# FFN gate and up in a transformer block: half of the k-tiles in pairs by a Strassen form, with sums of weights on GpSimd

## The chip, the cores and the metric

One core of a Trainium2 chip runs one launch of the kernel. The metric is the device time of the launch in microseconds (us), the median of the runs shown.

## The reference

One layer over 256 tokens of width 2,048, all in float32: an input projection, differential attention and a state-space branch side by side, a merge, an output projection, and then the part that the change touches, the feed-forward network (FFN):

```python
z = _rms_norm(h, norm_ffn_pre[l])
f = (jax.nn.silu(z @ w_ffn_gate[l]) * (z @ w_ffn_up[l])) @ w_ffn_down[l]
h = h + _rms_norm(f, norm_ffn_post[l])
```

`w_ffn_gate` and `w_ffn_up` are 2048 x 5632, `w_ffn_down` is 5632 x 2048.

## The kernel before

The kernel is a list of blocks (class `Block`). A block multiplies 256 tokens, as two halves t of 128, with weights that come in k-tiles of 128 rows and 1,024 columns. A weight tile is loaded in float32 (`do_load`, line 178), then split (`do_split`, line 191): ScalarE rounds it to fp32r, `hi`, and VectorE forms `lo` = raw - hi. Activations are split in the same way. A product is then three matmuls into one PSUM bank, hi x hi, hi x lo and lo x hi (`run_block`, line 254).

The FFN's gate and up are eleven blocks, ffn0 to ffn10 (lines 1266 to 1276). Block b takes columns 512 b to 512 b + 511 of both matrices: a raw tile holds 512 gate columns and beside them 512 up columns (`load_ffn`, line 1233), so it comes by two DMAs, or, where a tile for two k-tiles is used, by two larger ones. There are 16 k-tiles, two token halves and two column halves c (gate, up): 16 x 4 products, 192 matmuls of 128x512, in four accumulators of one bank each. `ffn_evac` (line 1243) takes Silu of the gate bank on ScalarE and multiplies with the up bank on VectorE; the root-mean-square factor of the norm is put in there, as a scale per token. `hid_t` (line 1257) transposes the result with eight matmuls per block into `hT`, which the block "down" reads.

What sets the order: `ensure` (line 210) asks, ahead of step i, for the splits up to step i + 4 and for loads up to eight further steps. There are five buffers each for hi and lo in this stage (three in `ring`, two in `late`), so split i + 5 uses the buffers of split i and can't start before TensorE is through with that. Raw tiles come from a ring of four, and at two places in eight from a pool of six large buffers (`big8`), as a tile for two k-tiles. From the ninth step of ffn0 on (`unpin`), a scheduler may move instructions within their engines; what it made of it is the order shown below. GpSimd has nothing to do in the eleven blocks but one small power (`make_rstd`, line 393).

The normalised activations are made at the end of the output projection and in ffn0: `h_transpose` (line 1176) puts transposed pieces into the scratch tile `ga`, `h_split` (line 1187) splits them into `zT`. PSUM has eight banks: four in the pool `acc`, two single ones in `side`, and one double one (`side2`).

```python
        A.copy(h, raws[i])
        V.tensor_tensor(l, raws[i], h.bitcast(F32), op=ALU.subtract)
```

Of the kernel before, what the change touches and what calls it, by code (L numbers as in the profile page):

```python
# [88 lines left out]
def hybrid_block_kernel(  # L89
# [85 lines left out]
    state = dict(loaded=0, split=0, cap=None)  # L175
    raws, his, los = {}, {}, {}

    def do_load(i):
# [12 lines left out]
    def do_split(i):
# [1023 lines left out]
    def norm2():  # L1215
# [9 lines left out]
        before={12: lambda: cap(wo1, 17, True), 13: lambda: cap(wo1, 17, True), 16: lambda: cap(wo1, 18), 17: lambda: h_transpose(0, 0)},  # L1225
        post=wo_post)
# [40 lines left out]
    for b in range(NB):  # L1267
        pre = None
        if b == 1:
            def pre():  # L1270
                w_ = big8()
                A.dma_start(w_, norm_ffn_post.broadcast_to([P, DM]))
                wpost2.append(w_)
        add(f"ffn{b}", 16, load_ffn(b), lz, ffn_evac(b), budget=0.6, pre=pre,
            )
    blocks[-NB].order = token_order(16, head=4)[:8] + bank_order(16)[4:]
# [148 lines left out]
```

## Time and profile before

| what | value |
|---|---|
| median of 3 runs | 1437.61 us (1437.18 to 1438.76) |
| the profiled execution | 1436.86 us |
| its span | 1435.1 us |
| busy share of the span | PE 96%, DVE 64%, ACT 47%, POOL 16% |
| granted clock of TensorE, mean | 0.985 |
| bytes moved by DMA | 266.7 MB, mean 186 GB/s |

PE is TensorE, DVE VectorE, ACT ScalarE, POOL GpSimd, SP SyncE, which issues most DMAs. The span is the time from the first to the last instruction of the execution that was profiled; the execution's own time is 1.8 us longer. Times in the views count from the start of the span. An instruction's listed time runs from its start on its engine to its end, a wait for a shared resource after the start included.

### The profile page before, as it was taken

Reading aid. Unit: us, or ns where it says so; the run is one execution under the profiler, and the core shown is the slowest. Engines: PE = TensorE matmul, PEld = TensorE weight load, DVE = VectorE, ACT = ScalarE, POOL = GpSimd, SP = SyncE. Lnnn points to the kernel's source line nnn. Section 1 sums busy time; section 2 is a strip of 40 time slices with the busy share of each in tenths; the row PEclk is TensorE's granted clock in tenths of the full one; section 3 lists DMA queues with packets and bytes.
Section 4 is the critical chain, followed back from the end, with each engine's and each line's share of the span. In section 5 each row is a group of like instructions: output and inputs, shape, how many; then the busy total and the mean of one; then the engine's idle time right before and its main releaser. Section 6 shows DMA issues by size and latency. Waiting matters only on the chain.

```text
span 1435.1 us, 17346 instructions
## 1 busy us (share of the span) xinstructions
PE 1375.7 (96%) x6367; PEld 1115.7 (78%) x6367; DVE 923.2 (64%) x1122; ACT 680.8 (47%) x989; POOL 232.9 (16%) x195
## 2 busy tenths in 40 slices
PE   8998898999899879999999999999999999999997
PEld 6887676668676659888788888888888888888885
DVE  5965999967999975754764444444444445555555
ACT  4654443497443354444464444444444435444443
POOL 3293545500645500000000000000000000000001
PEclk9999999999999999999999999999999999999999
DMA  8688555444456465655576555556565564555651
GB/s 259 187 263 253 171 175 154 141 132 140 154 158 176 145 184 207 227 197 191 188 238 202 197 182 196 176 191 205 176 199 185 175 211 171 204 200 182 205 176 59
DMA packets 102006, 266.70 MB, mean 186 GB/s; under 512 B 10176, under 2 KB 17168, under 8 KB 98528
## 3 DMA queue, kind: packets, MB, share of 16 engines
q1 hardware_dynamic: 100704, 260.09, 56.1%
q10 hardware_dynamic: 608, 4.20, 0.8%
q0 software_dynamic: 608, 1.30, 0.4%
q8 instruction: 50, 0.82, 0.2%
q14 instruction: 36, 0.29, 0.1%
HBM read 257.16 MB, written 8.39 MB: 185 GB/s over the span
## 4 chain that ended last, share of the span: by engine, by line
issue 55%; PE 23%; DVE 15%; ACT 3%; DMA 2%; SPq 1%; POOL 0%; POOLq 0%; DVEq 0%; ACTq 0%
PE acc L41 22%; DVE lo L41 4%; DVE ssA L41 2%; DVE ssB L41 2%; DVE ssD L41 2%; PE side L41 2%; DVE ssC L41 2%; DMA raw<-in_w_in_dram 1%; DVE sim L41 1%; ACT hi L41 1%; SPq L623 1%; DMA raw<-in_w_glu_dram 1%; ACT prob L41 1%; DVE sre L41 1%; DVE b L41 1%
## 5 line engine op out<-in xcount | busy, mean ns | idle before, releaser
L41 DVE TENSOR_TENSOR lo<-raw,hi 128x1024 fp32r<-128x1024 f32 (+1 forms) x341 | 439.7, 1294 | 246.5 <-ACT hi L41 243.0
L41 ACT CAST hi<-raw 128x1024 fp32r<-128x1024 f32 (+1 forms) x340 | 355.0, 1051 | 399.0 <-PE acc L41 316.8
L41 PE MATMUL acc<-lo,zT_h 128*128 128x512 f32 x704 | 275.1, 391 | 0.0
L41 PE MATMUL acc<-hi,zT_l 128*128 128x512 f32 x704 | 274.3, 390 | 0.0
L41 PE MATMUL acc<-hi,zT_h 128*128 128x512 f32 x704 | 271.2, 393 | 0.2 <-ACT zT_h L41 0.2
L41 DVE TENSOR_TENSOR lo<-b,hi 128x1024 fp32r<-128x1024 f32 x124 | 151.1, 1224 | 147.6 <-ACT hi L41 147.6
L41 PE MATMUL acc<-lo,xT_h 128*128 128x512 f32 x512 | 207.4, 408 | 14.1 <-DVE lo L41 14.1
L41 PE MATMUL acc<-hi,xT_l 128*128 128x512 f32 x512 | 202.0, 397 | 0.0
L41 ACT CAST hi<-b 128x1024 fp32r<-128x1024 f32 x124 | 130.6, 1053 | 120.4 <-PE acc L41 104.0
L41 PE MATMUL acc<-hi,xT_h 128*128 128x512 f32 x512 | 165.8, 407 | 5.8 <-ACT hi L41 4.1
L41 PEld LDWEIGHTS acc<-hi,zT_h 128*128 128x128 f32 x704 | 132.3, 188 | 27.6 <-ACT zT_h L41 0.7
L41 PEld LDWEIGHTS acc<-hi,zT_l 128*128 128x128 f32 x704 | 132.3, 188 | 27.6
L41 PEld LDWEIGHTS acc<-lo,zT_h 128*128 128x128 f32 x704 | 132.3, 188 | 26.5
L41 PEld LDWEIGHTS acc<-lo,xT_h 128*128 128x128 f32 x512 | 98.8, 193 | 44.2 <-DVE lo L41 22.4
L41 PEld LDWEIGHTS acc<-hi,xT_h 128*128 128x128 f32 x512 | 97.6, 194 | 29.2 <-ACT hi L41 5.1
L41 PEld LDWEIGHTS acc<-hi,xT_l 128*128 128x128 f32 x512 | 98.3, 192 | 20.1 <-issue 0.8
L398 POOL TENSOR_TENSOR rstdf<-rstdfm,half 128x1 f32<-128x1 f32 x2 | 1.1, 546 | 691.6 <-DVE rstdfm L41 691.6
L41 PE MATMUL acc<-hi,b 128*128 128x512 f32 x256 | 84.1, 403 | 1.3 <-DVE ga L41 1.0
L638 POOL TENSOR_TENSOR tabS<-tabs,tabc 128x512 f32<-128x512 f32 x16 | 46.9, 2932 | 143.9 <-DVE ssB L41 143.9
L41 PE MATMUL acc<-lo,hTh 128*128 128x512 f32 x176 | 68.5, 389 | 0.0
L41 PE MATMUL side<-lo,hTh 128*128 128x512 f32 x176 | 68.5, 389 | 0.0
L41 PE MATMUL side<-hi,hTh 128*128 128x512 f32 x176 | 68.5, 389 | 0.0
(209 smaller groups left out, 1796.0 us busy)
## 6 DMA issues: line engine op xcount, KB each, us to landing
raw<-in_w_in_dram SPq DMA_DIRECT2D x127, 512.0 KB, 3.9
raw<-in_w_ffn_gate_dram SPq DMA_DIRECT2D x96, 256.0 KB, 2.8
raw<-in_w_ffn_up_dram SPq DMA_DIRECT2D x96, 256.0 KB, 3.1
raw<-in_w_ffn_down_dram SPq DMA_DIRECT2D x44, 512.0 KB, 3.7
b<-in_w_ffn_down_dram SPq DMA_DIRECT2D x22, 1024.0 KB, 4.9
b<-in_w_ffn_gate_dram SPq DMA_DIRECT2D x40, 512.0 KB, 3.8
b<-in_w_ffn_up_dram SPq DMA_DIRECT2D x40, 512.0 KB, 4.7
raw<-in_w_out_dram SPq DMA_DIRECT2D x32, 512.0 KB, 4.1
```

Of the source, the lines that this page charges most:

```text
L41: ins = f(*a, **kw)
L398: G.tensor_tensor(r, ms, half[:, :n], op=ALU.pow)
L623: nc.sync.dma_start(stack_b[:, j // 2, n, :, j % 2].rearrange("g q o n -> q g o n"), t_[32 * j:32 * j + 32])
L638: G.tensor_tensor(tss, hi(sa), lo(cb), op=ALU.mult)
```

## The change

In ffn1 to ffn10 the 16 k-tiles become four groups of four: two direct tiles (D), and a pair. For a pair the products form a 2 x 2 matrix of blocks: rows are the token halves, the inner index is the two k-tiles, columns are gate and up. Instead of eight block products it uses seven, in the Strassen-Winograd form. They need four sums of weight blocks of 128x512, t1 = b12 - b11, t2 = b22 - t1, t3 = b22 - b12, t4 = b21 - t2, which GpSimd forms in half of `ga` (`do_sums`). What is split for a pair is R2 (the second raw tile, two products), B1 (the gate half of the first, one product), T13 (t1 and t3, two) and T24 (t2 and t4, two): 24 splits in a block, four of them half as wide, where there were 16. Direct tiles still have four products, though one of them uses the difference of the two token halves' activations, so that all tiles add into the same seven accumulators P1 to P7. `combos` forms the sums of activations, once, during ffn0. At a block's end `s_evac` makes the four results out of the seven banks with seven additions and a copy, then Silu and gating from SBUF. Seven of the eight banks are in use in a block; odd and even blocks lay them out differently (`s_alloc`). The other half of `ga` holds the raw pairs of every second group, the four ring buffers everything else, and `big8` loads are used no more in ffn1 to ffn10 nor in the first eight steps of down. The load of the last norm's weights moves from ffn1 to the ninth step of down.

```diff
     def do_split(i):
...
-        A.copy(h, raws[i])
-        V.tensor_tensor(l, raws[i], h.bitcast(F32), op=ALU.subtract)
+        if blk.sets and blk.sets[k][0] != "D":
+            kind, kk = blk.sets[k]
+            r1, r2 = blk.pairs[kk]
+            raw = dict(R2=r2, B1=r1[:, 0:512], T13=sums[:, 0:1024], T24=sums[:, 1024:2048])[kind]
+        else:
+            raw = raws.pop(i)
         his[i], los[i] = h, l
-        del raws[i]
+        h, l = h[:, 0:raw.shape[1]], l[:, 0:raw.shape[1]]
+        A.copy(h, raw)
+        V.tensor_tensor(l, raw, h.bitcast(F32), op=ALU.subtract)
+
+    def do_sums(i):
...
+        t1, t3, t2, t4 = (sums[:, 512 * n:512 * n + 512] for n in range(4))
+        G.tensor_tensor(t1, b12, b11, op=ALU.subtract)
+        if kind != "T24":
+            G.tensor_tensor(t3, b22, b12, op=ALU.subtract)
+        G.tensor_tensor(t2, b22, t1, op=ALU.subtract)
+        G.tensor_tensor(t4, b21, t2, op=ALU.subtract)
+        if kind == "T24":
+            G.tensor_tensor(t3, b22, b12, op=ALU.subtract)
 
     def ensure(i):
...
+        while state["summed"] <= min(hi_i + 2, len(flat) - 1, state["loaded"] - 1):
+            do_sums(state["summed"])
+            state["summed"] += 1
...
+    def combos(cb):
...
+        tt(z1[:, k0:k1], z0[:, k0:k1], z1[:, k0:k1], op=ALU.subtract)
+        tt(z1[:, k2], z1[:, k1], z1[:, k2], op=ALU.add)
+        tt(z1[:, k1], z0[:, k1], z1[:, k1], op=ALU.subtract)
+        tt(z0[:, k1], z1[:, k2], z0[:, k1], op=ALU.subtract)
+        tt(z0[:, k2], z0[:, k2], z0[:, k1], op=ALU.subtract)
+        (ch, cl), cd = hold["cs"], hold["cd"]
+        for src, h, l in ((z1[:, k0:k1], cd[:, 0, cb], cd[:, 1, cb]),
+                          (z1[:, k1:k1 + 2], ch[:, 0:2, cb], cl[:, 0:2, cb]),
+                          (z0[:, k1:k1 + 2], ch[:, 2:4, cb], cl[:, 2:4, cb])):
+            A.copy(h, src)
+            tt(l, src, h.bitcast(F32), op=ALU.subtract)
...
+    for q in range(4):
+        SETS += [("D", 4 * q), ("D", 4 * q + 1)]
+        SETS += [(kind, 4 * q + 2) for kind in (("R2", "B1", "T13", "T24") if q < 3 else ("T24", "B1", "T13", "R2"))]
+    USES = dict(D=(("P4", 0), ("P5", 1), ("P2", 0), ("P3", 1)), R2=(("P2", 0), ("P3", 1)), B1=(("P1", 0),),
+                T13=(("P7", 1), ("P5", 0)), T24=(("P6", 0), ("P4", 1)))
...
+    def s_evac(b):
+        def f(key, accs):
...
+            if key == "P1":
+                A.copy(s0, accs["P1"])
+                plus(X, s0, "P6")
+            elif key == "P7":
+                plus(Y, X, "P7")
+            elif key == "P5":
+                plus(X, X, "P5")
+            elif key == "P3":
+                plus(X, X, "P3")
+                plus(s1, Y, "P4")
+                plus(Y, Y, "P5")
+                plus(s0, s0, "P2")
+                gated(1, s1, Y)
+                gated(0, s0, X)
...
+    for b in range(1, NB):
+        add(f"ffn{b}", len(SETS), load_ffn(b), None, s_evac(b), budget=0.6, mm=s_mm, alloc=s_alloc(b),
+            order=[[(n, key, c) for key, c in USES[kind]] for n, (kind, _) in enumerate(SETS)])
+        blocks[-1].sets = SETS
```

How the instructions now stand on three engines follows. In the rows, `raw`, `ga` and `b` numbers tell buffers apart, and the brackets name the engines or DMA queues that a row waits for.

GpSimd, from the end of the state-space tables to the end of the program, before:

```order
L640 TENSOR_TENSOR tabS_4270<-tabS_4270,tabt_874_4271 128x512 [waits Pool_49]
L398 TENSOR_TENSOR rstdm_5910<-rstdmm_5908,half 128x1 [waits DVE_49]
L398 TENSOR_TENSOR rstdm_5953<-rstdmm_5951,half 128x1 [waits DVE_49]
L398 TENSOR_TENSOR rstdh_6251<-rstdhm_6249,half 128x2 [waits DVE_49]
L398 TENSOR_TENSOR rstdf_11152<-rstdfm_11150,half 128x1 [waits DVE_49]
```

GpSimd in ffn1 now, the four sums of one pair from ring buffers and of one from `ga`:

```order
L243 TENSOR_TENSOR ga<-raw_6457 128x512 [waits DMAHW5_49,DMAHW4_49,DVE_49]
L245 TENSOR_TENSOR ga<-raw_6458,raw_6457 128x512 [waits DMAHW7_49]
L246 TENSOR_TENSOR ga<-raw_6458,ga 128x512 [waits DVE_49,Pool_49]
L247 TENSOR_TENSOR ga<-raw_6458,ga 128x512 [waits DMAHW6_49,Pool_49]
L243 TENSOR_TENSOR ga<-ga 128x512 [waits DMAHW3_49,DMAHW2_49,DVE_49]
L249 TENSOR_TENSOR ga<-ga 128x512 [waits DMAHW1_49]
L246 TENSOR_TENSOR ga<-ga 128x512 [waits DVE_49,Pool_49]
L247 TENSOR_TENSOR ga<-ga 128x512 [waits DMAHW0_49,Pool_49]
```

Where GpSimd had no work between two norms it has 16 subtractions per block, and each group of sums waits for VectorE's splits of the group before, whose place in `ga` it takes.

VectorE at the end of ffn1, before (b is the tile of the gate values, acc the banks):

```order
L41 TENSOR_TENSOR lo_6615<-raw_6465,hi_6614 128x1024 [waits DMAHW3_49,DMAHW2_49,Activation_49]
L41 TENSOR_TENSOR lo_6637<-raw_6484,hi_6636 128x1024 [waits DMAHW5_49,DMAHW4_49,Activation_49]
L41 SCALAR_TENSOR_TENSOR b_1155_5959<-acc_6373,rstdh_6251,b_1155_5959 128x512 [waits PE_49,Activation_49]
L41 SCALAR_TENSOR_TENSOR b_1155_5959<-acc_6375,rstdh_6251,b_1155_5959 128x512 [waits PE_49,Activation_49]
L41 TENSOR_TENSOR lo_6641<-raw_6503,hi_6640 128x1024 [waits DMAHW7_49,DMAHW6_49,Activation_49]
L41 TENSOR_TENSOR lo_6691<-b_1248_6522,hi_6690 128x1024 [waits DMAHW1_49,DMAHW0_49,Activation_49]
```

VectorE at the end of ffn1 now (acc_6414 to acc_6417 are P4, P5, P2, P3; side_1220 holds P6 and P7; lo_6738, lo_6750 and lo_6783 are R2, B1 and T13 of the next block's first group):

```order
L41 TENSOR_TENSOR b_1046_5329<-b_1046_5329,side_1220_6413 128x512 [waits Activation_49]
L41 TENSOR_TENSOR lo_6738<-raw_6626,hi_6737 128x1024 [waits DMAHW6_49,DMAHW7_49,PE_49,Activation_49]
L41 TENSOR_TENSOR b_1046_5329<-b_1046_5329,acc_6416 128x512 [waits DVE_49,PE_49]
L41 TENSOR_TENSOR lo_6750<-raw_6625,hi_6749 128x512 [waits DMAHW4_49,Activation_49]
L41 TENSOR_TENSOR b_1046_5329<-b_1046_5329,side_1220_6413 128x512 [waits PE_49]
L41 TENSOR_TENSOR lo_6783<-ga,hi_6782 128x1024 [waits Activation_49]
L41 TENSOR_TENSOR b_1046_5329<-b_1046_5329,acc_6415 128x512 [waits DVE_49]
L41 TENSOR_TENSOR b_1046_5329<-b_1046_5329,acc_6414 128x512
L41 TENSOR_TENSOR b_1046_5329<-b_1046_5329,acc_6417 128x512 [waits DVE_49]
L41 TENSOR_TENSOR b_1046_5329<-b_1046_5329,acc_6415 128x512 [waits DVE_49]
L41 SCALAR_TENSOR_TENSOR b_1046_5329<-b_1046_5329,rstdh_6290 128x512 [waits DVE_49,Activation_49] x2
```

Two gatings from PSUM became seven additions from PSUM and two gatings from SBUF, and three of the additions stand between splits of the next block.

ScalarE in ffn2 between the two copies into hT and after, before:

```order
L41 COPY hT<-side_1270_6672 128x4x128 [waits PE_49]
L41 CAST hi_6706<-b_1248_6522 128x1024 [waits DVE_49,PE_49]
L41 CAST hi_6725<-b_1253_6557 128x1024 [waits DMAHW2_49,DMAHW3_49,DVE_49,PE_49]
L41 COPY hT<-side_1270_6672 128x4x128 [waits PE_49]
L41 CAST hi_6741<-b_1253_6557 128x1024 [waits DVE_49,PE_49]
L41 CAST hi_6760<-raw_6592 128x1024 [waits DMAHW4_49,DMAHW5_49,DVE_49,PE_49]
```

ScalarE at the same place now (hi_6807 is T24 of the first group, hi_6833 and hi_6843 the direct tiles of the second, hi_6873 and hi_6892 its T13 and T24, hi_6926 a direct tile of the third):

```order
L41 COPY hT<-side_6767 128x4x128 [waits PE_49]
L41 CAST hi_6807<-ga 128x1024 [waits PE_49,Pool_49]
L41 CAST hi_6833<-raw_6672 128x1024 [waits DMAHW4_49,DMAHW3_49,PE_49]
L41 CAST hi_6843<-raw_6691 128x1024 [waits DMAHW6_49,DMAHW5_49,PE_49]
L41 COPY hT<-side_6798 128x4x128 [waits PE_49]
L41 CAST hi_6926<-raw_6804 128x1024 [waits DMAHW1_49,DMAHW2_49,DVE_49,PE_49]
L41 CAST hi_6873<-ga 128x1024 [waits DVE_49,PE_49,Pool_49]
L41 CAST hi_6892<-ga 128x1024 [waits DVE_49,PE_49,Pool_49]
L41 CAST hi_6916<-raw_6779 128x1024 [waits DMAHW0_49,DMAHW7_49,DVE_49,PE_49]
```

Casts of sums wait for GpSimd, and hi_6926 was moved ahead of three casts of sets that come earlier in the block.

## Rows read from the trace of the kernel before

**Rows 1.** The page: busy time, share, instructions; granted clock in 40 slices.

```profile
PE 1375.7 (96%) x6367; PEld 1115.7 (78%) x6367; DVE 923.2 (64%) x1122; ACT 680.8 (47%) x989; POOL 232.9 (16%) x195
...
PEclk9999999999999999999999999999999999999999
```

**Rows 2.** Windows of ffn0 and of two later blocks, with granted clock and DMA.

```profile
core 0: us, PE busy (x) PEld busy (x) DVE busy (x) ACT busy (x) POOL busy (x), PEclk, DMA share, GB/s
692.80:737.30 44.50, 44.41 (x208) 36.42 (x209) 35.07 (x46) 26.18 (x44) 1.53 (x2) 1.00 0.74 252
780.77:825.26 44.49, 44.49 (x201) 36.84 (x200) 20.84 (x19) 19.32 (x21) 0.00 (x0) 1.00 0.56 189
825.26:869.75 44.49, 44.49 (x201) 36.85 (x200) 20.86 (x19) 19.32 (x21) 0.00 (x0) 1.00 0.58 189
```

**Rows 3.** Timeline of ACT: start, duration, instruction, idle time before it.

```profile
760.37 1.05 ACT L41 CAST hi<-raw 128x1024 fp32r<-128x1024 f32 x1 [1.67 <-DMA raw<-in_w_ffn_up_dram]
763.09 1.05 ACT L41 CAST hi<-b 128x1024 fp32r<-128x1024 f32 x1 [1.67 <-DMA raw<-in_w_ffn_up_dram]
...
780.77 0.69 ACT L41 ACTIVATE b<-acc,rstdh 128x512 f32<-128x512 f32 x1 [0.31 <-PE acc L41]
...
1136.66 0.69 ACT L41 ACTIVATE b<-acc,rstdh 128x512 f32<-128x512 f32 x1 [0.30 <-PE acc L41]
```

**Rows 4.** Groups of ffn1 to ffn10 (busy us, mean ns); DVE's timeline at 714.

```profile
L41 DVE TENSOR_TENSOR lo<-raw,hi 128x1024 fp32r<-128x1024 f32 x77 | 94.2, 1224 | 100.3 <-ACT hi L41 97.3 <-DMA b<-in_w_ffn_up_dram 3.0
L41 ACT CAST hi<-raw 128x1024 fp32r<-128x1024 f32 x78 | 82.3, 1055 | 113.4 <-PE acc L41 71.7 <-DMA raw<-in_w_ffn_up_dram 26.6 <-DMA b<-in_w_ffn_gate_dram 11.7
L41 DVE SCALAR_TENSOR_TENSOR b<-acc,rstdh,b 128x512 f32<-128x512 f32 x20 | 15.0, 751 | 24.5 <-PE acc L41 22.5 <-ACT b L41 2.0
...
714.11 2.35 DVE L41 TENSOR_TENSOR lo<-raw,hi 128x1024 fp32r<-128x1024 f32 x2
```

**Rows 5.** Timelines of DVE, then POOL, state-space stage, 443 to 457 us.

```profile
443.94 1.21 DVE L41 TENSOR_TENSOR lo<-raw,hi 128x1024 fp32r<-128x1024 f32 x1
445.08 0.68 DVE L41 TENSOR_TENSOR sre<-ssA,ssC 128x512 f32<-128x512 f32 x1
445.68 0.68 DVE L41 TENSOR_TENSOR ssD<-ssD,tabC 128x512 f32<-128x512 f32 x1
446.28 1.21 DVE L41 TENSOR_TENSOR lo<-raw,hi 128x1024 fp32r<-128x1024 f32 x1
447.42 0.68 DVE L41 TENSOR_TENSOR ssA<-side,tabC 128x512 f32<-128x512 f32 x1
...
448.88 2.08 DVE L41 TENSOR_TENSOR lo<-raw,hi 128x1024 fp32r<-128x1024 f32 x1
450.88 0.68 DVE L41 TENSOR_TENSOR ssB<-side,tabS 128x512 f32<-128x512 f32 x1
451.48 0.68 DVE L41 TENSOR_TENSOR ssC<-side,tabC 128x512 f32<-128x512 f32 x1
...
453.72 2.31 DVE L41 TENSOR_TENSOR lo<-raw,hi 128x1024 fp32r<-128x1024 f32 x1
...
444.10 4.31 POOL L638 TENSOR_TENSOR tabS<-tabs,tabc 128x512 f32<-128x512 f32 x1 [7.64 <-DVE ssB L41]
448.38 1.50 POOL L635 TENSOR_TENSOR tabC<-tabc,tabc 128x512 f32<-128x512 f32 x1
449.96 2.16 POOL L637 TENSOR_TENSOR tabC<-tabC,tabt 128x512 f32<-128x512 f32 x1
452.19 1.06 POOL L639 TENSOR_TENSOR tabt<-tabc,tabs 128x512 f32<-128x512 f32 x1
453.33 1.62 POOL L640 TENSOR_TENSOR tabS<-tabS,tabt 128x512 f32<-128x512 f32 x1
455.03 1.92 POOL L636 TENSOR_TENSOR tabt<-tabs,tabs 128x512 f32<-128x512 f32 x1
```

**Rows 6.** POOL's groups by shape: count, busy us, mean ns.

```profile
L638 POOL TENSOR_TENSOR tabS<-tabs,tabc 128x512 f32<-128x512 f32 x16 | 46.9, 2932 | 143.9 <-DVE ssB L41 143.9
...
L639 POOL TENSOR_TENSOR tabt<-tabc,tabs 128x512 f32<-128x512 f32 x16 | 22.1, 1380 | 1.2
```

**Rows 7.** DVE's 256-column split, and splits of 128 columns (min/median/max ns).

```profile
746.64 0.43 DVE L41 TENSOR_TENSOR hTl<-hT,hTh 128x256 fp32r<-128x256 f32 x1 [3.19 <-ACT hTh L41]
...
L41 DVE TENSOR_TENSOR zT_l<-ga,zT_h x10: 294/684/692, 692.8 to 724.4; 128x512 fp32r<-128x512 f32 x6, 128x128 fp32r<-128x128 f32 x2, 128x384 fp32r<-128x384 f32 x2
```

**Rows 8.** The page's DMA issues: KB each, median us to landing.

```profile
raw<-in_w_ffn_gate_dram SPq DMA_DIRECT2D x96, 256.0 KB, 2.8
raw<-in_w_ffn_up_dram SPq DMA_DIRECT2D x96, 256.0 KB, 3.1
```

More of the change, by code (lines that the diff above doesn't have):

```diff
@@ L54, in __init__ @@
         self.before = before or {}
+        self.sets, self.pairs, self.summed = None, {}, set()
 def bank_order(nk, head=1, tail=2):
@@ L174, in hybrid_block_kernel @@
     flat = []
-    state = dict(loaded=0, split=0, cap=None)
+    state = dict(loaded=0, split=0, summed=0, cap=None)
+    sums = ga[:, 0].rearrange("p a b -> p (a b)")
     raws, his, los = {}, {}, {}
@@ L180, in do_load @@
         blk, k = flat[i]
-        if late.get("ffn") and i % 8 in (4, 6):
+        if blk.sets:
+            kind, kk = blk.sets[k]
+            if kind == "D":
+                r = ring.tile([P, 1, 1024], F32, tag="raw", name=nm("raw"), bufs=4)
+                blk.load(kk, r)
+                raws[i] = r[:, 0, :]
+            elif kk not in blk.pairs:
+                if kk % 8 == 6:
+                    pair = [ga[:, 1, a, :].unsqueeze(1) for a in range(2)]
+                else:
+                    pair = [ring.tile([P, 1, 1024], F32, tag="raw", name=nm("raw"), bufs=4) for _ in range(2)]
+                for a, r in enumerate(pair):
+                    blk.load(kk + a, r)
+                blk.pairs[kk] = [r[:, 0, :] for r in pair]
+            return 1
+        if late.get("ffn") and i % 8 in (4, 6) and (blk.name != "down" or k >= 8):
             r = big8(shape=(P, 2, 1024))
@@ L1224, in hybrid_block_kernel @@
                                               [(14, 1, 1), (15, 1, 1)]],
[L1225 to L1226 removed]
+        before={12: lambda: cap(wo1, 17, True), 13: lambda: cap(wo1, 17, True), 16: lambda: cap(wo1, 18), 17: lambda: h_transpose(0, 0)})
     wo1 = blocks[-1]
@@ L1258, in hid_t @@
         for t in range(2):
-            ps = side4()
+            ps = side()
             sg = hid.pop((b, t))
@@ L1266, in hybrid_block_kernel @@
     NB = DFF // 512
[L1267 to L1276, printed above, removed]
+    add("ffn0", 16, load_ffn(0), lz, ffn_evac(0), budget=0.6)
+    blocks[-1].order = token_order(16, head=4)[:8] + bank_order(16)[4:]
@@ new lines, in s_alloc, with f @@
+    def s_alloc(b):
+        def f():
+            wide = side2()
+            acc = lambda: acc_pool.tile([P, 512], F32, tag="acc", name=nm("acc"))
+            d = {}
+            if b % 2:
+                for key in ("P4", "P5", "P2", "P3"):
+                    d[key] = acc()
+                d["P1"], d["P6"], d["P7"] = side(), wide[:, 0, :], wide[:, 1, :]
+            else:
+                d["P4"], d["P5"], d["P2"] = wide[:, 0, :], wide[:, 1, :], side()
+                for key in ("P3", "P1", "P6", "P7"):
+                    d[key] = acc()
+            return d
+        return f
@@ L1282, in steps @@
         return f
-    blocks[-NB].before = {
+    ffn0.before = {
         0: steps((cap, wo1, 19)), 3: steps((h_piece, 1, 0)),
@@ L1383, in dn_pre, with dn_weights @@
             drain(f"hid{b}")
-    bd = add("down", nck, load_dn, ldn, dn_evac, order=dn_order, alloc=dn_alloc, pre=dn_pre, ensure=down_ensure)
+    def dn_weights():
+        w_ = big8()
+        A.dma_start(w_, norm_ffn_post.broadcast_to([P, DM]))
+        wpost2.append(w_)
+    bd = add("down", nck, load_dn, ldn, dn_evac, order=dn_order, alloc=dn_alloc, pre=dn_pre, ensure=down_ensure,
+             before={8: dn_weights})
     bd.akey = lambda m: (m[1], m[2] + 2 * (m[0] % 2))
```

61 lines of the change are left out of this document (52 added, 9 removed).

## The prediction

> **What bounds the kernel now.** The page comes first: TensorE (PE) is busy 96% of the span and its granted clock is 9 in every slice, the upper of its two levels, 2.4 GHz [rows 1]. Next the windows, one FFN block each: from ffn1 on PE is busy in all of a block's 44.49 us, VectorE (DVE) in 20.8, ScalarE (ACT) in 19.3, GpSimd (POOL) in none, at clock 1.00 [rows 2]. The timeline of ACT gives the period: the first Silu of a block starts at 780.77, the same one eight blocks later at 1136.66, so 355.89 / 8 = 44.49 us. The cast of a k-tile follows the last one after 2.72 us, and a k-tile is 12 matmuls: 0.2267 us each. 192 of them are 43.53 us, and the other 0.96 are the eight transposes [rows 3]. So in ten blocks (444.9 us) PE alone sets the time, and fewer matmuls pay only while the engines that feed it stay below the block's time.
>
> **Matmuls.** In each of blocks 1 to 10 eight k-tiles keep 12 matmuls each (96), four pairs take 7 products of 3 instead of 24 matmuls (84): 180 for 192. Twelve times 0.2267 is 2.72 us per block, 27.2 in all; PE then needs 41.77 per block.
>
> **Splits.** A block had 16 splits into hi and lo, all 1,024 columns. It will have 8 for direct tiles and 4 each of R2, T13 and T24 (20 wide), and 4 of B1 at 512 columns. On ACT a wide cast takes 1.06 [rows 4]; 4.2 more of those, four half ones and one copy leave it near 28 of 44, and I cost that at nothing, beside PE. On DVE two subtractions in a row take 2.35 and one lists 1.22 [rows 4], so one costs 1.13; a 512-column one costs 0.60 (445.08 to 445.68) [rows 5].
>
> **Sums on POOL.** 16 subtractions of 128x512 per block, where POOL did nothing. The trace has that shape in the tables of the state-space stage, at means of 1.38 to 2.93 us [rows 6]. Were that all, 16 would be 22 to 47 us beside everything else. The spread has a cause that decides this case. Take 448 to 457 us on DVE and POOL [rows 5]. POOL's tabC ends at 449.88; the DVE split that had started at 448.88 ends at 450.96, 1.08 later, though it lists 2.08. The next POOL one lists 2.16 from 449.96 and ends at 452.12, 1.16 after that split. Then again: POOL ends 454.95, the split 456.03, POOL 456.95. Neither moves while the other works. But the two DVE operations at 450.88 and 451.48, with one input in PSUM, take their usual 0.68 while POOL works. So POOL and those DVE instructions whose inputs both lie in SBUF take turns, as on one port. Every lo split has both inputs in SBUF.
>
> **The port's sum, per block.** Splits 20 x 1.08 to 1.13 = 21.6 to 22.6; four halves 2.4; the two gatings, whose inputs move from PSUM to SBUF, between the 0.60 of a subtraction and the 0.75 that a gating lists [rows 4], 0.67 each, 1.3; sums 16 x 1.16 = 18.6. Together 43.9 to 44.9, middle 44.4. That is no less than the 44.49 of before, with PE's 41.77 below it: nearly all of the 27 us is lost to the port even if it never rests.
>
> **DVE's additions.** The block's end adds seven 128x512 additions from PSUM, 7 x 0.60 = 4.2. Beside a sum they are free, as at 450.88; without a sum beside them they keep DVE from its splits. All hidden: 44.4. None hidden: 48.6. The order puts three of them between splits of the next block, while its first sums are queued, and four behind the split of T13, when two more sums may run; that POOL finds all of these free just then is too much to hope. I take half, 2.1, and a period of 46.5, which is 2.0 over before: **+20 us** over ten blocks.
>
> **A wait from the order.** In block 2 ACT now casts a direct tile of the third group ahead of the T13 of the second, and DVE follows. There are five pairs of hi and lo, so that cast waits for PE to finish a set five sets back, and PE soon needs the T13 behind it. No row of before has it. It costs from nothing, if POOL uses the port meanwhile, to a cast and two splits, 1.06 + 2 x 1.08 = 3.2, in such a block. I take 0, since the two sums of that group fit there (2.3), and keep 3.2 for the far end.
>
> **PSUM.** A block now holds seven of eight banks. The next block's first product gets the bank of P2, freed by one DVE addition that stands two places ahead of the T13 split: 0.6 to at most a blocked split more, 1.8. PE still has three matmuls (0.68) left then. I take 0 of its own.
>
> **ffn0.** Four calls of combos add one DVE subtraction of 256 columns, four of 128 and three splits of 256 each: 4 x (0.43 + 4 x 0.29 + 3 x 0.43) = 11.5 us [rows 7]. DVE was busy 35.1 of 44.5 there [rows 2], so listed time passes the span, although overlap of about 0.08 per instruction brings it back to near 40. PE enters with four k-tiles split ahead, 10.9 us of cover. I take **+2**, between 0 and 10; what is lost is the lead with which ffn1 starts.
>
> **Loads.** Bytes stay; DMA engines are 0.58 busy in a block [rows 2] and a tile lands within 2.8 to 3.1 us [rows 8]. A pair's buffers now go back only after the sums, but a direct tile's buffer comes round six sets later (10 us), less 2.4 for its split: 8 against 3.1. Nothing. SyncE's queue has loads waiting for POOL ahead of others; that is covered by the same 8 us. The load of the last norm's weights moves from ffn1 to the ninth step of the down block, far before its use: nothing.
>
> **Sum.** The profiled execution took 1436.86 (span 1435.1 and 1.8 around it); with +20 and +2 it is 1458.9, and the median of three runs, 1437.61, lies 0.75 above it. I round to 1459.
>
> **A rule weighed.** POOL's tabS lists 4.31 us from 444.10, and only 1.0 of it lies behind the DVE operation from PSUM at 447.42: it sat through a run of four DVE instructions with both inputs in SBUF, not one [rows 5]. The Trainium skill (SBUF — State Buffer, Who interferes with whom) says that a VectorE instruction with two SBUF inputs contends with GpSimd's reads, and that whoever comes second blocks until the first is finished; by that the port would change hands after every instruction, and the sum would be rival B's. The trace agrees that they exclude each other and shows a longer wait than one instruction, which is for C.
>
> **The rivals.**
> - A: the sums fall into time in which the port is free, and PE sets the time. 10 x 41.77: 27.2 less, **1410**. Against it stands the port's own 43.9, above 41.77; only sums far shorter than any unblocked row (1.06) would give it. 0.04.
> - B, which ends on the other side: the port is packed. POOL and DVE alternate without a gap and all seven additions lie beside sums. 43.9 to 44.9 per block, -6 to +4, and ffn0 absorbed: **1432 to 1442**. It decides as soon as the period is under 44.49, so with at most 0.1 us of DVE time exposed at the middle of the port's sum. For it: the strict turns at 449 to 457. Against: DVE was mostly supplied there, while here a block ends with a chain of additions, Silu and gating. 0.15.
> - C: POOL is held through runs of splits (as at 444.10), the T13 split waits for its sums, no addition is hidden, and the order's wait is paid. 48.1 to 49.1 per block, up to 3.2 more, ffn0 up to 10: **1474 to 1525**. Against it: DVE stops by itself at T13, which hands the port to POOL. 0.18.
> That the change doesn't do what it says is excluded: the built program has 120 fewer matmuls and 160 more POOL instructions.
>
> **How the numbers follow.** My forecast, with half to most of the additions exposed and small waits, has 0.63 and holds 1443 to 1474. From 1437 (inside B) to 1487 (inside C) about 0.2 is left out: A, some 0.08 of B, some 0.08 of C. A measurement of this kernel tells about 0.2% (2.9 us) from no change. Faster: A and 0.09 of B, 0.13. Same: 0.06 of B and 0.02 of the forecast's edge, 0.08. Slower: 0.61 and C, 0.79.
>
> **What would show it.** In blocks 1 to 10: period near 46.5; PE with waits for lo and hi that were not there; POOL listing about 1.2 to 2.3 per sum, splits with both lengths, 1.2 and near 2.3; port time of splits, gatings and sums together over 0.9 of the period. Wrong would be: splits of 1.22 beside sums (A), a period under 44.5 (B), PE waits mostly at block ends of 5 us and more or sums of 3 us and more (C), or a loss of over 10 us in ffn0.

## The result, and the profile after

The change makes the kernel slower: 1482.09 us (1477.64 to 1482.6, four runs) against 1438.08 (1437.18 to 1438.76), a ratio of 1.030 with the interval 1.028 to 1.032. The forecast was 1459, in a range of 1437 to 1487: the sign was right and the size was not, +21 said and +44 measured. Executions in a second, slower state (one each of the kernels y3 and z4 below and of the first form of w3) are left out of the medians.

The profiled execution took 1482.6, with a span of 1480.8. Its page, busy time and granted clock, answers to [rows 1]:

```profile
PE 1377.8 (93%) x6247; PEld 1100.3 (74%) x6247; DVE 1141.4 (77%) x1304; ACT 743.8 (50%) x1091; POOL 546.4 (37%) x355
...
PEclk9999999999899999999999999999999999999999
```

PE has 120 matmuls fewer and is busy 2.1 us longer. Where the time went is read from PE's timeline, between the first products of the stages: before ffn0 +1.0 (over all the kernels below this start lies between 690.6 and 695.6 us, so it tells nothing), ffn0 47.4 to 50.0 (+2.6), ten blocks 444.9 to 485.0 (+40.2), down 250.1 to 252.0 (+2.0), together the span's +45.8. The forecast had 0, +2, +20 and 0. The ten blocks as one window, of before and then of the change:

```profile
740.16:1185.03 444.87, 444.87 (x2001) 368.43 (x2000) 209.47 (x183) 193.98 (x204) 0.00 (x0) 1.00 0.57 190
```

```profile
743.78:1228.81 485.03, 446.61 (x1881) 354.89 (x1881) 414.85 (x326) 253.57 (x293) 307.38 (x157) 0.95 0.55 172
```

The columns are those of [rows 2]. TensorE needs 417.7 us for its 1,800 matmuls and 80 transposes at the old pace (ten times the prediction's 41.77). It stands still for 38.4 and is busy 28.9 longer than its work needs, at a granted clock of 0.95. Block by block (windows from one block's first product to the next one's, ffn3 to ffn6):

```profile
838.90:891.10 52.20, 44.64 (x189) 34.08 (x188) 47.77 (x39) 25.88 (x31) 37.85 (x19) 0.97 0.60 188
891.10:935.40 44.30, 44.08 (x188) 35.93 (x189) 35.83 (x29) 24.34 (x29) 25.72 (x15) 0.96 0.51 160
935.40:989.40 54.00, 46.30 (x190) 35.36 (x188) 48.12 (x39) 26.88 (x32) 36.96 (x19) 0.95 0.56 181
989.40:1033.60 44.20, 44.20 (x188) 36.06 (x189) 36.89 (x29) 23.61 (x28) 26.89 (x15) 0.95 0.50 158
```

Even blocks take 44 to 46, odd ones 50 to 54. DVE's and POOL's work differ too (39 and 19 instructions against 29 and 15), since in an odd block PE is held up while those two already work for the next. The mean is 48.5, forecast 46.5.

The groups of the ten blocks show the turns on the port that the forecast counted on (busy us, mean ns, then idle time):

```profile
L41 DVE TENSOR_TENSOR lo<-raw,hi 128x1024 fp32r<-128x1024 f32 x99 | 192.2, 1971 | 17.6 <-ACT hi L41 17.3
...
L41 DVE TENSOR_TENSOR lo<-ga,hi 128x1024 fp32r<-128x1024 f32 x100 | 128.8, 1312 | 47.1 <-ACT hi L41 46.7
...
L246 POOL TENSOR_TENSOR ga<-raw,ga 128x512 f32<-128x512 f32 x19 | 43.1, 2266 | 0.0
...
L247 POOL TENSOR_TENSOR ga<-ga 128x512 f32<-128x512 f32 x20 | 32.0, 1601 | 1.6
```

A direct split lists 1.97 on average instead of 1.22 [rows 4]; a sum lists 1.27 at the least and 2.27 on average in the group that always takes turns. The longest sum of all is 2.34 (L243's maximum): no sum was kept waiting through a run of splits, as tabS had been [rows 5]. The waits of the same stretch (engine, line, waited for: us, times, longest):

```profile
POOL ga L243 <- DVE lo L41: 106.4, 38, 5.5
ACT hi L41 <- POOL ga L247: 72.2, 20, 5.8
ACT hi L41 <- PE acc L41: 65.0, 60, 4.5
DVE lo L41 <- ACT hi L41: 64.0, 36, 3.7
...
PE side L41 <- DVE b L41: 17.1, 5, 3.8
...
PE acc L41 <- DVE b L41: 8.2, 9, 2.0
PE acc L41 <- DVE lo L41: 6.7, 8, 1.3
```

PE's largest wait (the row `PE side L41 <- DVE b L41`) comes five times, once at the end of each odd block, 2.9 to 3.8 us long. Timelines of PE, DVE and POOL at the end of ffn5:

```profile
981.35 0.40 PE L41 MATMUL acc<-lo,b 128*128 128x512 f32 x1
...
987.05 0.80 PE L41 MATMUL side<-hi,b 128*128 128x512 f32 x1 [3.72 <-DVE b L41]
987.65 0.63 PE L41 MATMUL side<-lo,b 128*128 128x512 f32 x1
```

```profile
981.88 4.52 DVE L41 TENSOR_TENSOR lo<-raw,hi 128x1024 fp32r<-128x1024 f32 x2
986.33 0.68 DVE L41 TENSOR_TENSOR b<-b,side 128x512 f32<-128x512 f32 x1
```

```profile
980.91 2.21 POOL L243 TENSOR_TENSOR ga<-raw 128x512 f32<-128x512 f32 x1 [4.16 <-DVE lo L41]
983.08 2.24 POOL L245 TENSOR_TENSOR ga<-raw,raw 128x512 f32<-128x512 f32 x1
985.28 2.24 POOL L246 TENSOR_TENSOR ga<-raw,ga 128x512 f32<-128x512 f32 x1
```

PE wants to write the last product of P7 into the double bank, where P7 lies beside P6. P6 has not been read yet: its addition at 986.33 stands in DVE's queue behind two splits, and these take turns with three sums, 4.52 us where two alone take 2.35. The granted clock around that wait (980 to 1000 us, 5 us each):

```profile
980.00:985.00 5.00, 3.34 (x15) 2.41 (x13) 5.00 (x4) 3.58 (x5) 4.09 (x2) 1.00 0.53 158
985.00:990.00 5.00, 2.29 (x5) 1.42 (x6) 5.00 (x5) 2.29 (x3) 4.66 (x3) 0.70 0.66 211
990.00:995.00 5.00, 5.00 (x16) 3.89 (x15) 5.00 (x7) 0.73 (x1) 2.97 (x2) 0.61 0.55 172
995.00:1000.00 5.00, 5.00 (x25) 4.13 (x24) 2.38 (x4) 2.03 (x3) 0.00 (x0) 1.00 0.28 90
```

After the wait the granted clock falls from its upper level, 2.4 GHz, to the lower one, 1.2, for part of two windows (0.70 and 0.61): a matmul lists 0.63 at 987.65, where it listed 0.40 at 981.35, and from 990 to 995 PE starts 16 instructions in a window that is busy throughout, 25 in the next.

### The profile page after: what moved, and what is told of

Read it like the earlier page. It is cut to its first block, busy times and chain, and to the rows that moved or that the text cites. A ratio compares the mean times of both kernels' runs of the same rounds, so it can differ in the third digit from the quotient of the medians.

```text
span 1480.8 us, 17939 instructions
## 1 busy us (share of the span) xinstructions
PE 1377.8 (93%) x6247; PEld 1100.3 (74%) x6247; DVE 1141.4 (77%) x1304; ACT 743.8 (50%) x1091; POOL 546.4 (37%) x355
## 4 chain that ended last, share of the span: by engine, by line
PE 31%; issue 29%; DVE 25%; ACT 5%; POOL 5%; DMA 4%; SPq 1%; DVEq 0%; POOLq 0%; ACTq 0%
PE acc L41 25%; DVE lo L41 13%; PE side L41 5%; ACT hi L41 3%; DVE ssA L41 2%; DVE ssB L41 2%; DVE ssD L41 2%; POOL ga L246 2%; DVE ssC L41 2%; DMA raw<-in_w_in_dram 2%; DVE b L41 1%; POOL ga L247 1%; POOL ga L243 1%; DVE sim L41 1%; SPq L667 1%
## 5 line engine op out<-in xcount | busy, mean ns | idle before, releaser
L41 DVE TENSOR_TENSOR lo<-raw,hi 128x1024 fp32r<-128x1024 f32 (+1 forms) x385 | 568.0, 1489 | 160.6 <-ACT hi L41 159.8
L41 ACT CAST hi<-raw 128x1024 fp32r<-128x1024 f32 (+1 forms) x384 | 389.4, 1028 | 347.5 <-PE acc L41 275.0
L41 PE MATMUL acc<-hi,b 128*128 128x512 f32 x616 | 229.6, 412 | 9.5 <-DVE b L41 5.4
L41 PE MATMUL acc<-lo,xT_h 128*128 128x512 f32 x512 | 206.1, 405 | 15.5 <-DVE lo L41 15.3
L41 PE MATMUL acc<-hi,xT_l 128*128 128x512 f32 x512 | 201.6, 397 | 0.0
L41 DVE TENSOR_TENSOR lo<-ga,hi 128x1024 fp32r<-128x1024 f32 (+1 forms) x120 | 146.6, 1262 | 47.1 <-ACT hi L41 46.7
L41 ACT CAST hi<-ga 128x1024 fp32r<-128x1024 f32 (+1 forms) x120 | 114.0, 977 | 129.8 <-POOL ga L247 72.2
L41 PE MATMUL acc<-hi,xT_h 128*128 128x512 f32 x512 | 164.5, 404 | 7.4 <-ACT hi L41 6.1
L41 PEld LDWEIGHTS acc<-hi,b 128*128 128x128 f32 x616 | 121.9, 199 | 41.2 <-DVE b L41 5.2
L41 PEld LDWEIGHTS acc<-lo,xT_h 128*128 128x128 f32 x512 | 97.9, 191 | 45.6 <-DVE lo L41 24.3
L41 PE MATMUL acc<-lo,b 128*128 128x512 f32 x308 | 127.0, 412 | 1.6 <-DVE lo L41 1.4
L41 PEld LDWEIGHTS acc<-hi,xT_h 128*128 128x128 f32 x512 | 97.1, 193 | 30.9 <-ACT hi L41 8.2
L41 PEld LDWEIGHTS acc<-hi,xT_l 128*128 128x128 f32 x512 | 97.7, 191 | 20.1 <-issue 0.8
L41 PE MATMUL acc<-lo,zT_h 128*128 128x512 f32 x244 | 97.2, 400 | 5.3 <-DVE lo L41 5.3
L41 PE MATMUL acc<-hi,zT_l 128*128 128x512 f32 x244 | 95.7, 396 | 0.0
L41 PE MATMUL acc<-hi,zT_h 128*128 128x512 f32 x244 | 86.2, 402 | 5.5 <-DVE b L41 3.0
L243 POOL TENSOR_TENSOR ga<-raw 128x512 f32<-128x512 f32 x20 | 42.3, 2116 | 109.0 <-DVE lo L41 62.5
L41 DVE TENSOR_TENSOR lo<-b,hi 128x1024 fp32r<-128x1024 f32 x40 | 49.0, 1225 | 39.0 <-ACT hi L41 39.0
L41 PEld LDWEIGHTS acc<-lo,b 128*128 128x128 f32 x308 | 61.5, 200 | 16.6 <-DVE lo L41 4.0
```

Of the source, the lines that this page charges most:

```text
L41: ins = f(*a, **kw)
L243: G.tensor_tensor(t1, b12, b11, op=ALU.subtract)
```

## The experiments

"Ten blocks" is the time in the trace from the first product of ffn1 to the first behind the last of ffn10, counted in products. "Port" is the time per block in which POOL or a DVE instruction with both inputs in SBUF works (their union over the trace); what is left of a block is the port's rest. Times are medians, each beside the kernel before on the same chip (1435 to 1438).

| kernel | us | ratio (interval) | ten blocks | port |
|---|---|---|---|---|
| the change | 1482.1 | 1.030 (1.028 to 1.032) | 485.0 | 44.3 |
| x1 tiny sums | 1424.5 | 0.991 (0.989 to 0.993) | 431.6 | 31.8 |
| x2 bank | 1467.7 | 1.021 (1.019 to 1.023) | 468.5 | 44.3 |
| x3 sums on DVE | 1435.3 | 0.999 (0.998 to 1.001) | 440.0 | 37.0 |
| x4 bank and DVE | 1432.0 | 0.997 (0.996 to 0.998) | 436.1 | 37.1 |
| y1 three pairs, POOL | 1444.3 | 1.006 (1.005 to 1.008) | 447.2 | 38.3 |
| y2 three pairs, DVE | 1425.0 | 0.993 (0.991 to 0.994) | 430.9 | 32.8 |
| y3 two pairs, POOL | 1437.8 | 1.001 (1.000 to 1.002) | 442.0 | 32.3 |
| y4 before, 32 sums | 1539.5 | 1.072 (1.070 to 1.074) | 539.7 | 54.0 |
| y5 before, 16 sums | 1437.2 | 1.000 (0.999 to 1.001) | 444.8 | 37.0 |
| z1 P6 by ScalarE | 1475.7 | 1.027 (1.025 to 1.029) | 477.9 | 44.8 |
| z4 the same, DVE | 1435.2 | 0.999 (0.997 to 1.000) | 438.4 | 37.6 |
| w3 direct last | 1470.9 | 1.024 (1.022 to 1.025) | 477.6 | 44.7 |
| w4 the same, DVE | 1421.5 | 0.989 (0.988 to 0.991) | 428.8 | 36.8 |
| v0 pairs in the ring | 1494.2 | 1.040 (1.038 to 1.042) | 493.4 | 44.5 |
| v1 and two buffers for sums | 1502.3 | 1.045 (1.044 to 1.047) | 504.5 | 44.5 |

**Port or banks?** Four kernels: sums made small (the kernel leaves out seven eighths of each), one bank dealt out otherwise, sums moved to VectorE, and the last two together.

```diff
-        G.tensor_tensor(t1, b12, b11, op=ALU.subtract)
+        G.tensor_tensor(t1[:, 0:64], b12[:, 0:64], b11[:, 0:64], op=ALU.subtract)
...
```

> The sums on GpSimd cover 64 of their 512 columns (the rest of the sums is left out); every wait stays. Theory port: the turns of GpSimd and VectorE on one port set the block's period, so with 16 x 0.35 in place of 16 x 1.16 us the port needs about 32 us of a block, the period falls from 48.7 to 42 to 43 us and the time to 1420 to 1435. Theory bank: what sets the period is TensorE waiting at block ends for additions that free or release a PSUM bank, and the half clock that follows; the additions then stand behind two unblocked splits (2.3 us) and not two blocked ones (4.5), so about half of these waits stay: 45 to 46 us per block, 1445 to 1460.

```diff
-                d["P1"], d["P6"], d["P7"] = side(), wide[:, 0, :], wide[:, 1, :]
+                d["P7"], d["P6"], d["P1"] = side(), wide[:, 0, :], wide[:, 1, :]
```

> In odd blocks P7 gets the single side bank, and P1 shares the double one with P6, so that the last products of P7 no longer follow the addition that reads P6. The sums stay as they are. Theory bank: the waits of 2.9 to 3.8 us of TensorE in five blocks (17 us) go, and with them the half clock behind them (some 2 us each): 1452 to 1466. Theory port: the port needs 44 to 45 us of a block whatever TensorE waits for, and the waits come back at other places: 1470 to 1482.

```diff
-        G.tensor_tensor(t1, b12, b11, op=ALU.subtract)
+        V.tensor_tensor(t1, b12, b11, op=ALU.subtract)
...
```

> The same 160 sums on VectorE, none on GpSimd. VectorE then needs per block splits 25, gatings 1.3, sums 16 x 0.60 = 9.6 and additions 4.2, together 40 us, just under TensorE's 41.8. Theory port: 42 to 43 us per block, 1420 to 1435. Theory bank: the additions still stand behind splits, and now behind sums: 45 to 47 per block, 1443 to 1465.

> Both: P7 in the single bank in odd blocks, and the sums on VectorE. Theory port: as with the sums on VectorE alone, 1420 to 1435. Theory bank: lower than either part alone, 1415 to 1435, and by 10 us or more lower than with the sums on VectorE alone.

Small sums give 1424.5 with the order, the waits and the banks of the change in place; the same full sums on VectorE give 1435.3. So what costs the change 47 to 58 us is that POOL forms the sums at full length: not the Strassen form, the additions or the banks by themselves. Both edits free the port and shorten the time for which casts wait for a sum, so these two runs alone don't tell one from the other; the next pair of runs has sums that nothing reads. The bank edit alone gives 14.4 back, between what the two theories said; beside sums on VectorE it gives 3.3. It is thus a wait that the sums on POOL make long. In x2 the P7 wait at the block's end is gone, but now the next block's first product waits 3.0 to 3.1 there, for the double bank of P6 and P1:

```profile
978.42 0.50 PE L41 MATMUL side<-hi,zT_h 128*128 128x512 f32 x1 [3.04 <-DVE b L41]
```

The ten blocks of x2, and ScalarE's wait for sums in them:

```profile
743.02:1211.55 468.53, 437.29 (x1881) 349.56 (x1882) 417.19 (x327) 253.08 (x293) 306.24 (x157) 0.98 0.56 178
```

```profile
ACT hi L41 <- POOL ga L247: 74.4, 20, 5.8
```

Beside the change PE stands still 7.2 us less and is busy 9.3 less, at a clock of 0.98 instead of 0.95. The port works as long as before, 44.3 per block, and rests 2.6 instead of 4.2.

**The port by itself.** Subtractions that nothing reads, in the kernel before (two per raw tile; in y5 one).

```diff
+        if blk.name.startswith("ffn") and blk.name != "ffn0":
+            for n in range(2):
+                G.tensor_tensor(ga[:, 0, n, 512 * (i % 2):512 * (i % 2) + 512], raws[i][:, 0:512], raws[i][:, 512:1024],
+                                op=ALU.subtract)
         A.copy(h, raws[i])
```

> The kernel before with two subtractions of 128x512 on GpSimd for each raw tile of ffn1 to ffn10, 32 per block, whose results nothing reads; VectorE's and TensorE's work is as before. Port theory (splits and sums exclude each other): 16 x 1.13 + 32 x 1.16 = 55.2 us per block against 44.49, so +107, 1525 to 1560. If they only slowed each other's listed time and could overlap, GpSimd would need 32 x 1.06 = 34 us and VectorE 20.8 plus at most 18, both below 44.49: 1434 to 1442.

> The kernel before with one subtraction of 128x512 on GpSimd for each raw tile of ffn1 to ffn10, 16 per block as in the change, whose results nothing reads. Port theory (only what the sum has above TensorE's time costs anything): 16 x 1.13 + 16 x 1.16 = 36.6 us against 44.49, so no change: 1433 to 1440. Turn theory (each turn delays the split that TensorE waits for): a loss of 5 to 20 us, 1441 to 1456.

Windows of y4 (two blocks), then of y5 (one):

```profile
1003.61:1059.41 55.80, 48.05 (x201) 37.89 (x201) 33.73 (x19) 18.45 (x21) 55.80 (x33) 0.94 0.46 151
1059.41:1114.93 55.52, 48.95 (x200) 38.33 (x200) 34.21 (x19) 18.42 (x21) 55.52 (x33) 0.94 0.46 152
```

```profile
960.55:1005.04 44.49, 44.49 (x202) 36.83 (x200) 26.60 (x18) 19.33 (x21) 27.20 (x17) 1.00 0.59 190
```

With 32 sums these blocks take 55.5 to 55.8 (ffn3 to ffn10 55.3 on average; ffn1 still takes 44.5), and 55.2 was worked out from turns that exclude each other (16 x 1.13 + 32 x 1.16); POOL is listed as busy all of it, although its own work is 37 (32 x 1.16). With 16 the listed times grow too (DVE 20.86 [rows 2] to 26.60), and the time doesn't move. Nothing reads these sums; they can hold the kernel up by the port, and by the raw tiles that stay in use until they have run. 37 us of work would fit into 44.49 if it could lie beside the splits. Both agree with a port that only costs what its sum has above TensorE's time. The Trainium skill (SBUF — State Buffer, Who interferes with whom) says that the shared port pair is an exclusive lock; y4 agrees, at 55.3 for 55.2.

**Less work for the port.** Only three groups, or the two middle ones, keep their pair; the rest is direct, and in even blocks the single banks go to P1, P6, P7, P3.

```diff
+        if q not in PAIRED:
+            SETS += [("D", 4 * q + 2), ("D", 4 * q + 3)]
+            continue
...
-                for key in ("P3", "P1", "P6", "P7"):
+                for key in ("P1", "P6", "P7", "P3"):
```

> The last group of four k-tiles in each block is direct again, the other three keep their pair; sums stay on GpSimd. The bank order in even blocks is P1, P6, P7, P3, so that the next block's first products get banks that came free early. PE needs 183 x 0.2267 + 0.96 = 42.45 us per block. Port: 19 wide splits 20.5 to 21.5, three halves 1.8, gatings 1.3, 12 sums x 1.16 = 13.9: 37.5 to 38.5, below PE. Port theory (the port costs only what its sum has above PE): period 42.5 to 43.6, in all 1419 to 1434. Turn theory (every stretch in which splits and sums take turns delays PE, whatever the sum per block): period 45 to 47, 1445 to 1465.

> As the kernel with three pairs, but with the sums on VectorE. PE needs 42.45 us per block; VectorE needs 19 x 1.13 + 1.8 + 1.3 + 7 x 0.60 + 12 x 0.60 = 36. Period 42.5 to 43.2, in all 1417 to 1430. Port theory: within 5 us of the one with the sums on GpSimd, since there the port has room. Turn theory: 10 us or more below it.

> Only the two middle groups keep their pair, sums on GpSimd. PE needs 186 x 0.2267 + 0.96 = 43.13 us per block; port 18 wide splits 19.4 to 20.3, two halves 1.2, gatings 1.3, eight sums 9.3: 31.2 to 32.1. Port theory: PE's own period, 43.1 to 43.8, in all 1424 to 1434, above the kernel with three pairs. Turn theory: 44.5 to 46, 1440 to 1455, below the kernel with three pairs.

Three pairs with sums on GpSimd have a port sum of 38, and come to 44.7 per block; with sums on VectorE 43.1. The port theory had said that both are alike, and it is 19 us off. Two pairs with sums on GpSimd come to 44.2, where TensorE needs 43.1, and at 1437.8 lie between the two theories' ranges. So in this order sums on GpSimd also cost something below the limit. y5, whose sums nobody waits for, shows no such cost; that the chain from a pair's sums to the casts of T13 and T24 makes the difference is likely by that, and wasn't tried by itself. In y1 POOL also waited long for raw tiles, which may delay its sums:

```profile
POOL ga L243 <- DMA raw<-in_w_ffn_up_dram: 132.0, 10, 14.6
```

In y2 VectorE's sums waited 7.8 us for the same tiles. No run separates this from the chain.

**Banks again.** Two kernels go further than x2: z1 has x2's edit, another order of the banks in even blocks, and takes P6 out of PSUM on ScalarE; w3 puts the direct tiles behind the pairs, so that each block ends with 5.4 us of products for which no addition is needed. It also deals out the banks anew, reads P2 earlier at the block's end, and starts ffn1's first sums and loads later. z4 and w4 are the same with the sums on VectorE.

```diff
-                plus(X, s0, "P6")
+                A.copy(s1, accs["P6"])
+                V.tensor_tensor(X, s0, s1, op=ALU.add)
```

> The change with three edits at its PSUM banks and nothing else: in odd blocks P7 has a bank of its own and P6 shares the double one with P1; in even blocks the four single banks go to P1, P6, P7, P3 in this order; and P6 leaves PSUM by a copy on ScalarE (as P1 does), X being formed from two copies in SBUF. Every block keeps 16 sums on GpSimd; the port gets one addition more, 44.4 + 0.6 = 45.0 us per block. Bank theory (the odd blocks' surplus over the port's sum is TensorE waiting for a bank that a VectorE addition, standing behind splits that take turns, has yet to read): odd blocks come down to the even ones' 44 to 46, in all 1447 to 1458. Port theory (a bank's wait only shows the port's backlog; without it the backlog comes back as a wait for lo): odd blocks keep 48 or more, 1462 to 1475.

> The same bank edits with the sums on VectorE. TensorE needs 41.77 us per block and VectorE is busy in about 41. Bank theory: the waits of 1.2 to 1.5 at the end of even blocks go, period 42.0 to 43.0, in all 1418 to 1428. If VectorE's own work is the bound by now: 43.2 to 44, 1430 to 1437.

```diff
-        SETS += [("D", 4 * q), ("D", 4 * q + 1)]
         SETS += [(kind, 4 * q + 2) for kind in (("R2", "B1", "T13", "T24") if q < 3 else ("T24", "B1", "T13", "R2"))]
+        SETS += [("D", 4 * q), ("D", 4 * q + 1)]
...
+            keys = (("P4", "P2", "P5", "P3"), ("P6", "P5", "P4", "P7"), ("P2", "P4", "P5", "P3"), ("P5", "P6", "P4", "P7"))[b % 4]
...
+            for n, key in enumerate(("P2", "P3") if b % 2 else ("P6", "P7")):
+                d[key] = wide[:, n, :]
```

> The same order, banks and first steps with the sums on GpSimd: the port's sum is 44.4 us per block as in the change, and no block ends with additions that TensorE waits for. Bank theory: 44 to 46 per block, 1440 to 1455. Port theory: the backlog shows as waits for hi, lo and banks elsewhere, 47 to 49 per block, 1463 to 1478, as the run of this order with altered first sums gave.

> All four pairs, direct tiles behind their pair, the banks handed out anew, sums on VectorE; the first sums and the first pair's load of ffn1 are issued one and two steps later, behind the last of ffn0's combined activations. TensorE needs 41.77 us per block, VectorE about 41, and ffn0 loses nothing. If the end of the block was what held the version with the two edits (1432): 42 to 43.3 per block, 1418 to 1428. If VectorE's own work holds it: 1430 to 1437.

The ten blocks of w3, then of w4:

```profile
743.22:1220.85 477.63, 440.25 (x1882) 344.20 (x1880) 421.53 (x331) 255.47 (x295) 309.50 (x158) 0.99 0.56 177
```

```profile
739.36:1168.17 428.81, 422.16 (x1882) 344.47 (x1880) 404.75 (x485) 257.83 (x295) 1.35 (x1) 1.00 0.62 195
```

Both z1 and w3 come to a mean of 47.8 per block, and the bank theory had said 44 to 46: it falls. Odd and even are alike in z1 and mixed in w3 (45.5 to 51.0). In z1 the wait is there again, 2.8 to 3.1 us some 7 us into each of ffn2 to ffn10, for another bank, whose addition stands behind the same turns:

```profile
987.91 0.50 PE L41 MATMUL acc<-hi,b 128*128 128x512 f32 x1 [2.93 <-DVE b L41]
```

In w3 PE's waits lie all over the block, for splits (10.5 us), additions (12.2) and casts (13.9). With 16 sums on GpSimd none of four arrangements (the change, x2, z1, w3) came under 46.85 per block. z4 takes 1435.2, no less than x4. The order of w3 with the sums on VectorE takes 42.9 per block, 1.1 above TensorE's need, and beats both kernels: 1421.5 against 1437.1. (A first form of w3 and w4 formed ffn1's first sums over activations that ffn0 still had to combine, so some of ffn1's data differed; it took 1469.9 and 1424.9.)

**Why does the port rest?** In the change it is free for 4.2 us per block, 41.9 in all. Of these 8.3 lie under DVE's additions from PSUM. Another 11.2 are ten rests of 1.1, one in each block: POOL stands still, and DVE waits while ScalarE casts a new sum.

```profile
976.78 3.47 ACT L41 CAST hi<-ga 128x1024 fp32r<-128x1024 f32 x4 [5.80 <-POOL ga L247]
```

```profile
977.87 4.10 DVE L41 TENSOR_TENSOR lo<-ga,hi 128x1024 fp32r<-128x1024 f32 x4 [3.64 <-ACT hi L41]
```

And 14.7 are five rests of 2.2 to 3.7, one in each even block, where the cast that DVE waits for itself waits for TensorE, which has yet to free a buffer of hi:

```profile
803.03 1.57 ACT L41 CAST hi<-ga 128x1024 fp32r<-128x1024 f32 x2 [4.27 <-PE acc L41]
```

```profile
804.11 1.23 DVE L41 TENSOR_TENSOR lo<-ga,hi 128x1024 fp32r<-128x1024 f32 x1 [3.47 <-ACT hi L41]
```

These five are gone in x2, the ten of 1.1 are not: its rest is 25.7 in all, 16.2 less, and its ten blocks are 16.5 shorter. So the wait for a bank at the end of an odd block comes back as rest of the port in the next.

v1 tries a second buffer for the sums, at the cost of raw buffers for two of the pairs; v0 is its control.

```diff
-                if kk % 8 == 6:
-                    pair = [ga[:, 1, a, :].unsqueeze(1) for a in range(2)]
...
+    sets2 = [sums, ga[:, 1].rearrange("p a b -> p (a b)")]
...
-        t1, t3, t2, t4 = (sums[:, 512 * n:512 * n + 512] for n in range(4))
+        t1, t3, t2, t4 = (sets2[kk % 8 == 6][:, 512 * n:512 * n + 512] for n in range(4))
```

> A control: the change with the raw tiles of all four pairs in the ring of four buffers (two of the four pairs had a place of their own in ga). Work and order are the same; loads get less lead. If the loads have room: as the change, 1478 to 1488. If the ring now holds them up: up to 1 us per tile that comes late, 1488 to 1520.

> As the control, and the place in ga that came free is a second buffer for the sums, so that GpSimd need not wait for the splits of one pair's sums before it forms the next pair's. Hand-over theory (in the change the port rests 4.2 us per block, 3.3 of them while ScalarE casts a new sum and GpSimd may not yet write the next ones): the rest shrinks to 1 to 2, 2 to 3.5 us per block less, 20 to 35 below the control. Bank theory, or GpSimd having nothing to do then anyway because the next raw tiles or the turn of the order are not there: within 8 of the control.

v1 is 8 us slower than its control, where 20 to 35 less was expected if the sums' buffer made the port rest. Its first row of waits tells why nothing can be said of the buffer:

```profile
POOL ga L241 <- DMA raw<-in_w_ffn_up_dram: 132.4, 26, 8.5
```

With fewer raw buffers POOL waits for loads (84.9 in the control, which is itself 12 us slower than the change), so the sums couldn't run ahead. A second buffer with the loads left as they were wasn't tried: whether it would shorten the ten rests of 1.1 stays open.

## Why the prediction was wrong in its size

The mechanism that the forecast was built on, one port for the sums and the splits, came as said. The loss was twice what it said, chiefly since waits for PSUM banks were put at nothing: one edit at a bank (x2) gives back 14.4 of the 23 us that the forecast was short. That 1482 lies inside the stated range is owed to the room left for rival C, whose mechanism did not come.

- **Matmuls** and **what bounds the kernel**: 120 fewer, as said, and no gain from them as long as the sums share the port. y5 and y4 confirm the reading of [rows 5] that the whole forecast stood on.
- **The port's sum**, 43.9 to 44.9 per block: right. Measured 44.3 (48.5 less 4.2 of rest).
- **DVE's additions**, "I take half, 2.1": mis-sized. 0.8 per block were exposed. So the forecast's 2.1 of rest and the measured 4.2 are made of different things.
- **PSUM**, "I take 0 of its own": the step that failed. It looked only at P2's bank and the next block's first product. The wait that came is for the double bank that P6 and P7 share in odd blocks, 2.9 to 3.8 us five times, behind splits that take turns; PE stood still for 5.8 to 7.7 us in each odd block and at most 1.2 in an even one. With P7 in a bank of its own (x2) a block takes 46.85, where the forecast had 46.5: 1.65 of the 2.0 us per block that were missing. The five long rests of the port go with it. It isn't a cost of its own, though: beside sums on VectorE the same edit is worth under a quarter of it (3.3 for 14.4 us).
- **A wait from the order**, "I take 0": right for the cast it names. In ffn2 the direct tile of the third group is cast at 808.31 without a wait, and the T13 right behind it, and PE is idle for 0.2 us in all of that block:

```profile
808.31 1.05 ACT L41 CAST hi<-raw 128x1024 fp32r<-128x1024 f32 x1
809.26 1.05 ACT L41 CAST hi<-ga 128x1024 fp32r<-128x1024 f32 x1
```

- The hand-over from a pair's sums to ScalarE's cast had no term: the ten rests of 1.1 us, 1.1 per block. ScalarE's whole wait for L247's sums, 72 us in 20 waits, is no measure of it, since x2 has 74 in 20 with a rest of 2.6. That the buffer of the sums is the cause wasn't shown: v1 didn't test it.
- The clock had no term. In the ten blocks PE was busy 28.9 us more than its work needs, at 0.95; in x2 19.6 more, at 0.98; in w4 4.5 more, at 1.00. In w3 it was 22.5 more at 0.99, so the clock is not all of it. How much would be left if PE's waits stayed and the clock didn't fall wasn't tried.
- **ffn0**, +2: measured +2.6, but for another reason. Most of it is one wait of ffn1's first product, 2.29 us for a bank that ffn0's Silu still reads (the row below); with the banks of w3 and w4 ffn0 takes 47.6 to 48.0 against 47.4, with the same combined activations in it.

```profile
743.78 0.50 PE L41 MATMUL acc<-hi,zT_h 128*128 128x512 f32 x1 [2.29 <-ACT b L41]
```

- **Loads**, 0: as said (2.8 and 3.0 to 3.1 us to landing, as in [rows 8]). Down's +2.0 had no term; with the banks and the order of w3 and w4 it is 0.3, and no run tells more.
- The rivals: A and B are excluded by the time. C had the time (1474 to 1525) and PE's waits at block ends, but not by its mechanism: the longest sum of 2.34 shows no hold through runs of splits, and most additions were hidden (0.8 of 4.2 exposed).

## What to carry to other kernels

Here, moving two-input work from a full engine to GpSimd did not unload VectorE, since both read SBUF: add their times up as one engine's, and compare that with the bound, before counting what the other engines gain. Beside that sum, look for every PSUM bank whose reader stands in VectorE's queue behind such work, double banks with two readers first: the turns nearly doubled the time in front of the reader (4.52 us for 2.35). The same 16 sums cost 49 us less on VectorE (w3, w4), in an order that ends each block with products that need no sum, and 47 less in the order of the change.

## What the runs showed that was not expected

- Even where the port's sum is 4 us below TensorE's time (y1: 38 against 42.45), the sums of pairs cost 1.6 us per block against the same sums on VectorE, while sums that nothing reads (y5) cost nothing.
- An engine that takes turns is listed as busy while it is blocked: POOL 55.52 of 55.52 us in y4 for 37 us of work. The listed busy times of POOL and DVE can't be added up where they contend (55.5 and 34.2 there, in a block of 55.5); their union tells how long the port works.
- In y4, too, PE waited (its busy time is 48 to 49 of 55.5 to 55.8 us) and the granted clock of the blocks was 0.94; in y5, with no waits, 1.00.
